# Keeping all engines of the first layer in source order, and taking its softmax one tile at a time, in a two-layer encoder on one core

## The chip, the core and the metric

The kernel runs on one core of a Trainium2 chip. A core has TensorE (PE, matrix products; its weight loads are listed as PEld), VectorE (DVE), ScalarE (ACT), GpSimd (POOL) and SyncE (SP), which here only issues transfers. All but SP and the transfers work from on-chip memory; each engine has its own list of instructions, and semaphores tie the lists together. The metric is the device time of one execution, in microseconds (us); lower is better.

## The reference

Input x has 512 tokens of 1024 features, in fp32. Two layers follow one another, each with its own weights:

```python
def reference(x, ...):
    for i in range(2):
        hn = rms_norm(x, norm_gain[i])
        y = mixer_a(hn, ...) if i == 0 else mixer_b(hn, ...)
        x = x + y
```

`mixer_a` projects hn to q, k and v for three dilation groups and to a gate, 16 heads of 64. q and k are normalised a head at a time. Each group is a window attention with a bias by relative distance (dilations 1, 4 and 16; 64 places of the group on each side). The three softmaxes are merged by their denominators, so that they can be computed as one softmax over all keys of the three groups. The result times silu(gate) goes through an output projection. `mixer_b` has one attention over a neighbourhood of an 8 x 64 grid with a bias in two dimensions, and the same gate and output projection.

## The kernel before

**Products.** Work goes by eight head pairs ("hc" in the code). A weight tile of up to 128 x 1024 fp32 (`wraw`, 8 slots) is loaded from HBM by SP, 512 KB at a time; some are first added to another one (POOL's adding DMA, line 184, or DVE, line 177). `split` (line 130) makes a high part `wh` (cast on ACT, line 133) and a low part `wl` (subtraction on DVE or POOL by turns, line 137), and a product is three matmuls, high x high, high x low and low x high (`mm3`, line 294). A job is the 128 x 512 piece of weights that one split gives: six matmuls of 512 columns in a `product`, or twelve at some places. `splits` keeps four splits queued ahead of the job that TensorE works on. Activations are split in the same way (hn_h and hn_l, and for the four sums and differences of quarters of hn in `mix`, mix_h and mix_l). From the second head pair on, projections are made from seven instead of eight block products (`main_a`): first the b11 product, then gate and v0 of the pair before, four products on mixed operands, and b21, with DVE and ACT adding the parts into rawq and rawk.

**Attention of layer A** (`attn_a`) for one pair, in the order of the code: q and k are turned (`tp`, `k_a`, `q_a`). Two passes (`scores(0)`, `scores(1)`) make scores ("log") of four tiles each. For each tile DVE adds the bias and takes minima (lines 935 and 946, into `p` and `mn`; the trace has four instructions for it), ACT takes exponents (959), DVE the reciprocal (769), ACT the normalisation (770), and DVE turns the tile in blocks of 32 into `pt` (883). SP then moves sixteen blocks, four at a time (`move`, line 891), so that probabilities lie transposed. `v_a` turns v; `bias_a` loads the next pair's bias (e<-l_d); `weigh` makes the products with v ("o"), and DVE multiplies the gate by them (790). A `y` tile goes to HBM and is read back and split at the end (yr<-y_d, 795 and 801).

**What sets the order.** TensorE's list is in source order. The source itself is woven: `main` yields after each block of matmuls, and `run` then calls `side` (the attention, startup and end work) until a due time. Time here is `clock`, a sum of the source's own estimates of the matmuls' lengths, in nanoseconds of TensorE. `later_on(d, job)` puts a job d further on; `yield d` lets the side rest for d; `yield "wait", key, d` rests until d after `stamp[key]`. All other engines' lists are put in order by a scheduler that simulates the program, except for the instructions wrapped in `tc.keep_in_program_order`, which stay in source order against each other. So the place of a DVE instruction need not be that of the source.

The relative bias of layer B is loaded at hc = 2 (`bias_rows`, 534), and its `fill` comes later by a timer of 4000 (537 to 542). At the start, `row_scale` ends the norm of layer A; then `scale_x`, `first_out` (head norms of the first q), `bias_lines`, `mix` and `q_a(0)` follow in `side`, while `main` goes through the first pair's projections.

Of the kernel before, what the change touches and what calls it, by code (L numbers as in the profile page):

```python
# [46 lines left out]
def tile_hybrid_encoder(  # L47
# [23 lines left out]

    def sb(t, off, dims):
        return bass.AP(t.tensor, t.offset + off, [t.ap[0]] + dims)
# [20 lines left out]
    nc.vector.memset(ones.bitcast(F32), 1.0)  # L94
    one = cp.tile([P, 1], F32, name="one")
    nc.vector.memset(one, 1.0)
# [14 lines left out]
    def rsqrt(eng, r, ss, n, scale):  # L111
# [6 lines left out]
        for _ in range(3):  # L118
            eng.tensor_mul(a[:, :n], r, r)  # L119
            if eng is nc.vector:  # L120
                eng.scalar_tensor_tensor(a[:, :n], a[:, :n], -0.5, v[:, :n], op0=ALU.mult, op1=ALU.mult)
                eng.scalar_tensor_tensor(r, a[:, :n], 1.5, r, op0=ALU.add, op1=ALU.mult)  # L122
                continue
# [6 lines left out]
    def split(raw, n):  # L130
        h = wp.tile([P, 512], F32R, tag="wh", name="wh", bufs=6)[:, :n]
        l = wp.tile([P, 512], F32R, tag="wl", name="wl", bufs=5)[:, :n]
        nc.scalar.copy(h, raw)  # L133
        turn[0] += 1
        a, b = pool[0]
        eng = nc.gpsimd if turn[0] * a % b < a else nc.vector
# [13 lines left out]
    class Plan:  # L150
# [28 lines left out]
        def add(self, at, dst, off):  # L179
# [4 lines left out]
                lambda: nc.gpsimd.dma_start(dst.tile, src(), accum_op=ALU.add)  # L184
            )

        def mixed(self, hc):
# [10 lines left out]
            for i in range(2):  # L198
                self.add(j + (2 if late else 3) + 2 * i, b11[i], b12[i].off)
                self.sum(j + (9 if late else 11) + 2 * i, t2[i], b11[i], b22[i], nc.vector)  # L200
# [48 lines left out]
    def load(raw):  # L249
# [4 lines left out]
        if not begun:  # L254
            nc.sync.dma_start(dst[:, :512], src[:, :512])
            begun.append(load_x(1, 2))
            dst, src = dst[:, 512:], src[:, 512:]
        nc.sync.dma_start(dst, src)
# [82 lines left out]
    def project(stat_h, stat_l, n, evac, guard, need=None, after=None):  # L341

        acc = {i: ps_acc.tile([P, 512], F32, tag="acc", name="acc") for i in range(4)}
        for k in range(KT):
# [11 lines left out]
            if after:  # L356
                yield ("xn",)
# [10 lines left out]
    def squares(v, ss, i, ns, on_act=True):  # L368
        sq = wk.tile([P, 512], F32, tag="sq", name="sq")[:, : ns * 64]
        if on_act:  # L370
            nc.scalar.activation(sq, v, AF.Square)  # L371
        else:
            nc.gpsimd.tensor_mul(sq, v, v)
        nc.vector.tensor_reduce(  # L374
            ss[:, i * ns : (i + 1) * ns], sq.rearrange("p (a b) -> p a b", b=64), axis=AX.X, op=ALU.add
        )
# [3 lines left out]
    def head_norm(raw, ss, ns, held):  # L380
# [3 lines left out]
        rsqrt(nc.vector, rs[:, : 4 * ns], ss[:, : 4 * ns], 4 * ns, 1.0 / DH)  # L384

        def scale():
            for i in range(4):
                by = rs[:, i * ns : (i + 1) * ns].unsqueeze(2).to_broadcast([P, ns, 64])
                v = raw[:, i, : ns * 64].rearrange("p (a b) -> p a b", b=64)
                m = nc.vector.tensor_mul(v, v, by)  # L390
                if held:
                    tc.keep_in_program_order(m)

        if held:
            later.append(scale)
        else:
            scale()
# [25 lines left out]
    def row_scale(ssq):  # L423

        rsqrt(nc.vector, rs_n, ssq, 4, 1.0 / D)
# [4 lines left out]
    def load_x(k0, k1):  # L430
        nc.sync.dma_start(x_all[:, k0:k1, :], xt[:, k0:k1, :])

    warm = cp.tile([P, 1], F32, name="warm")
    nc.vector.memset(warm, 0.0)
    nc.scalar.activation(warm, warm, AF.Exp)
    load_x(0, 1)
    nc.scalar.dma_start(ng, norm_gain)
# [12 lines left out]
    nc.scalar.dma_start(hg, head_gain)  # L450
    gk = cp.tile([P, 4], F32, name="gk")
    for i, (a, b) in enumerate(((0, 3), (1, 4), (2, 5), (6, 7))):
        nc.vector.scalar_tensor_tensor(
# [3 lines left out]
    def norm(layer, k, xk):  # L457
# [3 lines left out]
        nc.scalar.activation(h, xk, AF.Copy, scale=g)  # L461
        return nc.vector.scalar_tensor_tensor(l, xk, g, h.bitcast(F32), op0=ALU.mult, op1=ALU.subtract)

    def square_a(k):
# [3 lines left out]
        nc.scalar.activation(sq, x_all[:, k, :], AF.Square)  # L468
        if k:
            nc.gpsimd.tensor_add(st["ssq"], st["ssq"], sq)  # L470

    def scale_x():


        pa = spread()
        for k in range(KT):
            xk = x_all[:, k, :]
            nc.vector.scalar_tensor_tensor(xk, xk, ng[:, 0, k : k + 1], pa, op0=ALU.mult, op1=ALU.mult)

    def renorm(k):  # L480
        nc.scalar.copy(hn_h[:, k, :], x_all[:, k, :])
        (nc.gpsimd if k % 2 else nc.vector).tensor_sub(hn_l[:, k, :], x_all[:, k, :], hn_h[:, k, :].bitcast(F32))

    def mix():
# [6 lines left out]
        def put(n, src, eng):  # L491
            nc.scalar.copy(mix_h[:, n], src)
            eng.tensor_sub(mix_l[:, n], src, mix_h[:, n].bitcast(F32))

        nc.vector.tensor_sub(a, x21, x22)
        put(0, a, nc.gpsimd)
        yield 3000
        nc.vector.tensor_sub(b, a, x11)
        put(1, b, nc.vector)
        yield 4000  # L500
        nc.vector.tensor_add(b, b, x12)
# [940 lines left out]
```

## Time and profile before

| | |
|---|---|
| runs of the kernel before | 893.46 us median of three (890.31, 893.46, 900.19) |
| profiled execution | 896.53 us, its span 894.8 us |
| granted TensorE clock, mean | 0.973 |
| TensorE busy | 847.5 us, 95% of the span, 6611 matmuls |
| DVE busy | 650.4 us, 73% |
| ACT busy | 510.1 us, 57% |
| POOL busy | 311.4 us, 35% |
| data moved | 131.98 MB, 148 GB/s over the span |

Times of rows count from the start of the span. Layer A is 0 to about 594 us, layer B the rest. "Granted clock" is the share of TensorE's full speed that the chip's throttle let it have in that stretch; a stretch at 0.50 does half the work. In rows, "[x <-E]" says that the engine was idle for x us before the instruction, and that E ended this; "<-issue" is idle time for which the profile shows nothing. SPq rows are DMA issues, and their length is that of issuing, not of the transfer. All matmuls stand under the helper's line 288 and transposes under 292, so that they are told apart by the tiles' names.

### The profile page before, as it was taken

To read this page: it belongs to the slowest core of one execution; us is meant where nothing else is said; L and a number is where in the kernel's file an instruction comes from. 1 tells how busy PE (TensorE), PEld (TensorE's weight loads), DVE (VectorE), ACT (ScalarE), POOL (GpSimd) and SP (SyncE) were. 2 spreads that over 40 slices of the span, in tenths; PEclk is the share of its full clock that TensorE was granted. 3 is DMA by queue.
4 is the path that set the end of the run, shared out by engine and by line. 5 is a ranking of instruction groups with operands and counts; after the bars stand their busy time and mean duration, and the time that the engine had idled before them with its cause. 6 is when DMAs were issued, how large, how long until landed. Compare 5 with 4: busy or idle time off the path is not lost.

```text
span 894.8 us, 18174 instructions
## 1 busy us (share of the span) xinstructions
PE 847.5 (95%) x6611; PEld 700.7 (78%) x6611; DVE 650.4 (73%) x1641; ACT 510.1 (57%) x1066; POOL 311.4 (35%) x271
## 2 busy tenths in 40 slices
PE   9988999989997999989999898999999999999998
PEld 7766878868876778668878676778998988889776
DVE  6888995867866896886886886538576677766643
ACT  7656755835934845845845846436366446664540
POOL 6473442533432353343343334002222233222411
PEclk9998999989998999999999998989999999999999
DMA  9354575575474477475476472256235665455212
GB/s 344 117 109 101 134 198 127 122 219 129 115 210 141 107 187 185 106 218 141 107 200 180 105 235 80 65 172 215 95 127 138 168 185 156 136 146 146 92 48 95
DMA packets 56170, 131.98 MB, mean 148 GB/s; under 512 B 7184, under 2 KB 24528, under 8 KB 55952
## 3 DMA queue, kind: packets, MB, share of 16 engines
q1 hardware_dynamic: 49744, 108.78, 38.5%
q0 software_dynamic: 6048, 22.02, 14.6%
q8 instruction: 52, 0.85, 0.4%
q14 instruction: 38, 0.31, 0.1%
q10 hardware_dynamic: 288, 0.01, 0.0%
HBM read 111.73 MB, written 11.72 MB: 138 GB/s over the span
## 4 chain that ended last, share of the span: by engine, by line
PE 67%; DVE 11%; ACT 9%; DMA 6%; issue 4%; POOL 1%; SPq 1%; DVEq 0%; ACTq 0%; POOLq 0%
PE acc L288 55%; PE o L288 4%; PE log L288 4%; PE tp L292 4%; DVE wl L137 3%; DMA wraw<-in_w 2%; ACT p L770 2%; ACT p L1238 2%; ACT p L959 2%; DMA rp<-in_rpb 1%; ACT wh L133 1%; DVE rs L122 1%; DMA yr<-y_d 1%; DVE na L119 1%; ACT rawk L579 1%
## 5 line engine op out<-in xcount | busy, mean ns | idle before, releaser
L137 POOL TENSOR_TENSOR wl<-wraw,wh 128x512 fp32r<-128x512 f32 (+1 forms) x167 | 218.5, 1323 | 450.0 <-PE acc L288 229.3
L133 ACT CAST wh<-wraw 128x512 fp32r<-128x512 f32 (+1 forms) x360 | 210.0, 593 | 162.7 <-PE acc L288 141.8
L137 DVE TENSOR_TENSOR wl<-wraw,wh 128x512 fp32r<-128x512 f32 (+1 forms) x193 | 159.8, 830 | 66.3 <-PE acc L288 35.8
L288 PE MATMUL acc<-wh,hn_h 128*128 128x384 f32 (+1 forms) x488 | 190.1, 389 | 6.4 <-DVE rawq L657 2.3
L288 PE MATMUL acc<-wl,hn_h 128*128 128x384 f32 (+1 forms) x488 | 180.1, 369 | 0.6 <-DVE wl L137 0.4
L288 PE MATMUL acc<-wh,hn_l 128*128 128x384 f32 (+1 forms) x488 | 180.3, 369 | 0.0
L288 PEld LDWEIGHTS acc<-wh,hn_h 128*128 128x128 f32 x488 | 94.2, 193 | 26.5 <-issue 5.1
L288 PEld LDWEIGHTS acc<-wh,hn_l 128*128 128x128 f32 x488 | 93.7, 192 | 10.8 <-issue 0.4
L288 PEld LDWEIGHTS acc<-wl,hn_h 128*128 128x128 f32 x488 | 94.5, 194 | 9.2 <-DVE wl L137 0.9
L288 PE MATMUL acc<-wh,mix_h 128*128 128x512 f32 x224 | 89.6, 400 | 3.2 <-ACT wh L133 3.2
L288 PE MATMUL acc<-wl,mix_h 128*128 128x512 f32 x224 | 88.7, 396 | 2.8 <-DVE wl L137 1.7
L288 PE MATMUL acc<-wh,mix_l 128*128 128x512 f32 x224 | 88.2, 394 | 0.0
L288 PE MATMUL acc<-hn_h,wh 128*128 128x512 f32 x192 | 79.1, 412 | 0.2
L288 PE MATMUL acc<-hn_h,wl 128*128 128x512 f32 x192 | 75.4, 393 | 0.0
L288 PE MATMUL acc<-hn_l,wh 128*128 128x512 f32 x192 | 75.3, 392 | 0.0
L959 ACT ACTIVATE p<-p,mn 128x512 f32<-128x512 f32 (+1 forms) x64 | 44.9, 702 | 44.9 <-DVE mn L946 44.9
L770 ACT ACTIVATE p<-p,mn 128x512 f32<-128x512 f32 (+3 forms) x128 | 69.6, 588 | 0.0
L184 POOL DMA_DIRECT2D wraw<-in_w x42 | 37.3, 887 | 70.3 <-PE tp L292 17.9
L374 DVE TENSOR_REDUCE ss<-sq 128x4 f32<-128x256 f32 (+1 forms) x96 | 48.0, 503 | 16.3 <-ACT sq L371 8.9
L288 PE MATMUL acc<-y_h,wh 128*128 128x512 f32 x128 | 52.9, 414 | 4.1 <-ACT gt L610 4.0
L288 PEld LDWEIGHTS acc<-wh,mix_h 128*128 128x128 f32 x224 | 42.4, 189 | 14.2 <-ACT wh L133 4.3
L288 PEld LDWEIGHTS acc<-wl,mix_h 128*128 128x128 f32 x224 | 42.4, 189 | 13.3 <-DVE wl L137 3.2
(159 smaller groups left out, 1478.7 us busy)
## 6 DMA issues: line engine op xcount, KB each, us to landing
wraw<-in_w SPq DMA_DIRECT2D x95, 512.0 KB
wraw<-in_w POOLq DMA_DIRECT2D x42, 512.0 KB, 6.6
wraw<-in_w SPq DMA_DIRECT2D x38, 384.0 KB
pt<-pt SPq DMA_DIRECT2D x112, 64.0 KB
td<-tr SPq DMA_DIRECT2D x24, 224.0 KB
pt<-td SPq DMA_DIRECT2D x24, 224.0 KB
e<-l_d SPq DMA_DIRECT2D x32, 112.0 KB
e<-l_d SPq DMA_DIRECT2D x16, 128.0 KB
```

Source lines behind the costliest of these rows:

```text
L119: eng.tensor_mul(a[:, :n], r, r)
L122: eng.scalar_tensor_tensor(r, a[:, :n], 1.5, r, op0=ALU.add, op1=ALU.mult)
L133: nc.scalar.copy(h, raw)
L137: eng.tensor_sub(l, raw, h.bitcast(F32))
L184: lambda: nc.gpsimd.dma_start(dst.tile, src(), accum_op=ALU.add)
L288: nc.tensor.matmul(o, l, r, **kw)
L292: nc.tensor.transpose(o, i, ident)
L374: nc.vector.tensor_reduce(ss[:, i * ns : (i + 1) * ns], sq.rearrange("p (a b) -> p a b", b=64), axis=AX.X, op=ALU.add)
L579: nc.scalar.activation(dst, src, AF.Copy, scale=rs_n[:, i : i + 1])
L770: nc.scalar.activation(pr, pr, AF.Copy, scale=mn[:, 3:4])
L959: nc.scalar.activation(row, row, AF.Exp, bias=mn[:, 1:2], scale=-1.0, accum_out=mn[:, 2:3])
L1238: nc.scalar.activation(pr[:, o : o + n], pr[:, o : o + n], AF.Exp, bias=mn[:, 0:1], scale=-1.0, accum_out=mn[:, 2:3])
```

## The change

Four wrappers `vec`, `act`, `pol` and `syn` stand in for the engines everywhere. While `held[0]` is true, each instruction that goes through one of them is also kept in source order. It is set after the first `row_scale` and cleared when `main` has issued the last product of layer A:

```diff
+    held = [False]
+    class Ordered:
+        def __getattr__(self, name):
+            f = getattr(self.engine, name)
+            def call(*args, **kw):
+                m = f(*args, **kw)
+                return tc.keep_in_program_order(m) if held[0] else m
+            return call
+    vec, act, pol, syn = (Ordered(e) for e in (nc.vector, nc.scalar, nc.gpsimd, nc.sync))
...
     def main():
         for hc in range(NHC):
             yield from main_a(hc)
+        held[0] = False
```

As the list is then what the source says, the source now spells out the distance between steps that depend on one another, by timers and yields. The softmax goes a tile at a time:

```diff
-        def finish(hd, t, pr, row, mn):
-            normalise(row, mn)
-            turn(hd, t, pr, 4)
+        def least(n, tile_):
+            pr, row, mn = minima(*tile_)
+            later_on(1500, partial(exponents, row, mn))
+            later_on(2900, partial(normalise, row, mn))
+            later_on(3900, partial(turn, *tile_[:2], pr, 4))
         for u in range(2):
-            for n, (hd, t, pr, row, mn) in enumerate(scores(u)):
-                later_on(1300 * n, partial(exponents, row, mn))
-                later_on(1300 * n + 1300, partial(finish, hd, t, pr, row, mn))
+            for n, tile_ in enumerate(scores(u)):
+                later_on(400 + 900 * n, partial(least, n, tile_))
             if u:
                 stamp["scored", hc] = 0
                 for n in range(4):
-                    later_on(8500 + 1000 * n, partial(move, n))
-            yield 9500
+                    later_on(8000 + 2000 * n, partial(move, n))
+            yield 8500
         yield from v_a(hc)
-        yield "wait", ("pt", hc), 3000
+        yield "wait", ("pt", hc), 2500
         st["e", hc + 1] = bias_a(hc + 1)
-        yield "wait", ("pt", hc), 12500
+        yield "wait", ("pt", hc), 7500
```

Head norms (the reduce in `squares`, the squares themselves, the scales, `normed`) and the turns before the scores:

```diff
+        later_on(800, add) if held[0] else add()
+        later_on(800, partial(squares, *args)) if held[0] else squares(*args)
+            later_on(600 + 600 * i, partial(scale, i)) if held[0] else scale(i)
+        later_on(3000, go) if held[0] else go()
-        yield "wait", ("rawk", hc), 12000 if 0 < hc < NHC - 1 else 14000
+        yield "wait", ("rawk", hc), 8000 if hc < NHC - 1 else 11000
-        yield "wait", ("rawq", hc), 9000 if hc else 24000
+        yield "wait", ("rawq", hc), 8000
```

At the start, `scale_x` and `first_out` are woven together, a stamp each part, and `mix` comes before `bias_lines`; the products on mixed operands wait for the part that they use:

```diff
-        scale_x()
-        stamp["xn",] = 0
-        yield "wait", ("first",), 500
-        first_out()
-        yield 3000
-        bias_lines()
+        xs, parts = scale_x(), None
+        next(xs)
+        yield "wait", ("first",), 300
+        parts = first_out()
+        for _ in range(4):
+            next(parts)
+            yield 700
+            next(xs)
+            yield 700
+        next(parts, None)
+        for _ in xs:
+            yield 700
+        yield from mix()
+        yield from bias_lines()
         st["e", 0] = bias_a(0)
-        yield 2000
-        yield from mix()
-        stamp["mix",] = 0
         yield from q_a(0)
```

Beside that, `q_a` yields between its copies and subtractions, `mix` yields 1000 between its steps, the tiles of sums (`ss`) have three buffers instead of two, and `fill` is kept in order like the rest. The number of instructions on each engine is the same. Layer B's order is the scheduler's as before.

Where the instructions stand now is shown at three places. First SP at the third pair (hc = 2). Rows are transfers, destination <- source; `wraw` are weights, e0 and e12 the next pair's bias, `pt0<-pt` the moves. Before:

```order
L258 DMA wraw_2728<-in_w 128x1024
L810 DMA e0_2820<-l0_d_87 128x1x256 x2
L815 DMA e12_2821<-l12_d_88 128x1x224 x4
L891 DMA pt0_2431<-pt_98 32x512 x12
L258 DMA wraw_2771<-in_w 128x1024
L891 DMA pt0_2431<-pt_98 32x512 x4
L258 DMA wraw_2797<-in_w 128x1024
L258 DMA wraw_2835<-in_w 128x1024
L258 DMA wraw_2857<-in_w 128x1024
```

And after (L85 is the wrapper's call):

```order
L85 DMA wraw_2728<-in_w 128x1024
L85 DMA pt0_2434<-pt_98 32x512 x8
L85 DMA wraw_2767<-in_w 128x1024
L85 DMA pt0_2434<-pt_98 32x512 x4
L85 DMA wraw_2793<-in_w 128x1024
L85 DMA pt0_2434<-pt_98 32x512 x4
L85 DMA wraw_2821<-in_w 128x1024
L85 DMA e0_2837<-l0_d_87 128x1x256
L85 DMA e12_2838<-l12_d_88 128x1x224 x2
L85 DMA e0_2837<-l0_d_87 128x1x256
L85 DMA e12_2838<-l12_d_88 128x1x224 x2
L85 DMA wraw_2857<-in_w 128x1024
```

The moves stand ahead of the bias loads now, with a weight load between groups of four; before, they stood behind the bias loads, and four weight loads followed behind them in one run.

Second, DVE in the second pass of the same pair, from the last minima to the last turn (ISA is a minima instruction, STREAM_TRANSPOSE the turn). Before:

```order
L769 RECIPROCAL mn_2620<-mn_2620 128x1
L769 RECIPROCAL mn_2624<-mn_2624 128x1
L137 TENSOR_TENSOR wl_2670<-wraw_2502,wh_2669 128x512
L769 RECIPROCAL mn_2628<-mn_2628 128x1
L769 RECIPROCAL mn_2633<-mn_2633 128x1
L643 TENSOR_TENSOR rawq_2641<-acc_2642,rawk_158 128x512
L883 STREAM_TRANSPOSE pt_98<-p_2619 128x4x4x32
L643 TENSOR_TENSOR rawq_2641<-acc_2643,rawk_158 128x512
L883 STREAM_TRANSPOSE pt_98<-p_2623 128x4x4x32
L883 STREAM_TRANSPOSE pt_98<-p_2627 128x4x4x32
L137 TENSOR_TENSOR wl_2705<-wraw_2056,wh_2704 128x512
L883 STREAM_TRANSPOSE pt_98<-p_2632 128x4x4x32
```

And after:

```order
L85 ISA mn_2668 128x1
L85 RECIPROCAL mn_2633<-mn_2633 128x1
L85 TENSOR_TENSOR rawq_2622<-acc_2623,rawk_158 128x512
L85 TENSOR_TENSOR rawq_2622<-acc_2624,rawk_158 128x512
L85 STREAM_TRANSPOSE pt_98<-p_2632 128x4x4x32
L85 RECIPROCAL mn_2648<-mn_2648 128x1
L85 TENSOR_TENSOR wl_2701<-wraw_2056,wh_2700 128x512
L85 RECIPROCAL mn_2656<-mn_2656 128x1
L85 STREAM_TRANSPOSE pt_98<-p_2647 128x4x4x32
L85 RECIPROCAL mn_2668<-mn_2668 128x1
L85 STREAM_TRANSPOSE pt_98<-p_2655 128x4x4x32
L85 STREAM_TRANSPOSE pt_98<-p_2667 128x4x4x32
```

Before, the four reciprocals follow the four tiles' minima, and the turns stand together behind them. Now the first tile's turn stands ahead of the second tile's reciprocal, and the low part wl_2701 between two reciprocals.

On ACT at the same place (ACTIVATE p,mn is an exponent, ACTIVATE p a normalisation). Before:

```order
L959 ACTIVATE p_2619,mn_2620<-p_2619,mn_2620 128x512
L959 ACTIVATE p_2623,mn_2624<-p_2623,mn_2624 128x512
L621 COPY vt_2638<-vt_2638 128x64
L133 CAST wh_2669<-wraw_2502 128x512
L959 ACTIVATE p_2627,mn_2628<-p_2627,mn_2628 128x512
L959 ACTIVATE p_2632,mn_2633<-p_2632,mn_2633 128x512
L770 ACTIVATE p_2619<-p_2619,mn_2620 128x512
L770 ACTIVATE p_2623<-p_2623,mn_2624 128x512
L133 CAST wh_2684<-wraw_2502 128x512
L770 ACTIVATE p_2627<-p_2627,mn_2628 128x512
L133 CAST wh_2704<-wraw_2056 128x512
L770 ACTIVATE p_2632<-p_2632,mn_2633 128x512
```

And after:

```order
L85 ACTIVATE p_2632,mn_2633<-p_2632,mn_2633 128x512
L85 CAST wh_2660<-wraw_2483 128x512
L85 ACTIVATE p_2647,mn_2648<-p_2647,mn_2648 128x512
L85 ACTIVATE p_2632<-p_2632,mn_2633 128x512
L85 CAST wh_2679<-wraw_2483 128x512
L85 ACTIVATE p_2655,mn_2656<-p_2655,mn_2656 128x512
L85 ACTIVATE p_2667,mn_2668<-p_2667,mn_2668 128x512
L85 ACTIVATE p_2647<-p_2647,mn_2648 128x512
L85 CAST wh_2700<-wraw_2056 128x512
L85 ACTIVATE p_2655<-p_2655,mn_2656 128x512
L85 ACTIVATE p_2667<-p_2667,mn_2668 128x512
L85 CAST wh_2716<-wraw_2056 128x512
```

Exponents and normalisations of different tiles now alternate, and each cast has a fixed place among them; wh_2700, which wl_2701 above needs, stands behind two exponents and the normalisation of p_2647.

Third, DVE where the gate of the third pair meets the bias of layer B. Before:

```order
L390 TENSOR_TENSOR rawq_2641<-rawq_2641,rs_2889 128x512 x4
L537 TENSOR_SCALAR rp_3176<-rp_3176 128x248
L540 COPY lb_3218<-rp_3176 128x128
L790 TENSOR_TENSOR gt_2379<-gt_2379,o_2937 128x4x32
L790 TENSOR_TENSOR gt_2379<-gt_2379,o_2938 128x4x32
L790 TENSOR_TENSOR gt_2379<-gt_2379,o_2939 128x4x32
L790 TENSOR_TENSOR gt_2379<-gt_2379,o_2940 128x4x32
L662 TENSOR_TENSOR rawk_158<-rawk_158,acc_2700 128x512
```

And after, from the gate products on, and then where `fill` is:

```order
L85 TENSOR_TENSOR wl_2884<-wraw_2698,wh_2883 128x512
L85 TENSOR_TENSOR gt_2379<-gt_2379,o_2897 128x4x32
L85 TENSOR_TENSOR gt_2379<-gt_2379,o_2898 128x4x32
L85 TENSOR_TENSOR gt_2379<-gt_2379,o_2899 128x4x32
L85 TENSOR_TENSOR gt_2379<-gt_2379,o_2900 128x4x32
L85 TENSOR_REDUCE ss_2243<-sq_2890 128x8
```

```order
L85 TENSOR_TENSOR wraw_3218<-wraw_2698,wraw_2869 128x1024
L85 SCALAR_TENSOR_TENSOR gt_3192<-eg_3193,gt_3192 128x256
L85 TENSOR_TENSOR wl_3240<-wraw_2698,wh_3239 128x512
L85 TENSOR_SCALAR rp_3208<-rp_3208 128x248
L85 MEMSET lb_3299 128x376
L85 COPY lb_3299<-rp_3208 128x128
```

`fill` (rp, lb) stood ahead of the gate products (gt<-gt,o), and stands some forty rows behind them now, in the next pair's first pass.

317 lines of the change are left out of this document (163 added, 154 removed).

## The prediction

> **What bounds the kernel now.** I read the times first, then busy time by stage, TensorE's waits, and last the timeline around each wait.
>
> The stages (start:end, length, busy time and instructions of PE, PEld, DVE, ACT and POOL, granted clock, DMA share, GB/s):
> ```profile
> 58.00:594.00 536.00, 499.48 (x4641) 401.82 (x4642) 411.64 (x992) 318.83 (x618) 203.53 (x166) 0.96 0.56 145
> 424.20:486.10 61.90, 61.51 (x590) 50.07 (x590) 52.09 (x127) 40.63 (x79) 25.13 (x21) 1.00 0.66 169
> 486.10:562.00 75.90, 68.89 (x599) 54.97 (x599) 54.92 (x126) 46.34 (x84) 29.86 (x23) 0.93 0.48 136
> 436.00:459.00 23.00, 22.81 (x102) 18.61 (x102) 20.08 (x48) 17.69 (x36) 12.65 (x10) 1.00 0.57 132
> 594.00:895.00 301.00, 293.75 (x1749) 256.42 (x1747) 192.63 (x581) 153.66 (x387) 75.54 (x81) 1.00 0.47 140
> 509.40:512.80 3.40, 3.40 (x9) 2.49 (x10) 3.40 (x5) 3.28 (x7) 2.64 (x3) 0.50 0.26 88
> ```
> TensorE bounds it. The edit ends at 594, so all that it can win lies in the first row: 536.0 − 499.5 = 36.5 us idle, and a granted clock of 0.96, about 21 to 24 us of full speed (24 by adding up the stretches at 0.50, of 3.4 or 6.8 us, each worth half its length). Some 60 us in all. The second row is a head pair in which nothing is lost (0.4 us idle); the third one in which much is.
>
> What TensorE waits for between 0 and 594 (engine, line <- releaser: us, times, longest):
> ```profile
> PE tp L292 <- DVE gt L790: 7.0, 1, 7.0
> PE o L288 <- issue: 6.9, 2, 3.7
> PE tp L292 <- DVE rawq L390: 5.1, 1, 5.1
> PE acc L288 <- ACT gt L610: 4.0, 1, 4.0
> PE acc L288 <- ACT wh L133: 3.2, 2, 2.2
> PE acc L288 <- ACT rawk L579: 2.1, 1, 2.1
> PE acc L288 <- DVE wl L137: 2.1, 5, 0.7
> PE o L288 <- DMA pt<-pt: 2.1, 2, 1.4
> PE acc L288 <- POOL wl L137: 1.1, 2, 0.9
> ```
> Few and long: six accidents, not a steady rate. Each has its own cause, so I price them one by one; what follows an idle stretch at half clock is added to it.
>
> **The gains.** *The relative bias (7.0 + 3.4 of clock).* DVE row, then the load's issue on SP:
> ```profile
> 273.37 0.29 DVE L537 TENSOR_SCALAR rp<-rp 128x248 f32<-128x248 f32 x1 [10.07 <-DMA rp<-in_rpb]
> 260.29 0.58 SPq L534 DMA_DIRECT2D rp<-in_rpb  x1
> ```
> The load was issued behind five weight loads and landed 13.1 us later; DVE stood before it for 10.1 us, with the gate products behind it. In the changed order `fill` stands after the gate products, and its load behind one weight load: at 13.1 / 5 = 2.6 us for each of the five it lands after some 3 to 5 us, against the 4 that the timer allows and the rows of DVE between. 0 to 2 us of DVE may stay, behind which weight parts stand that are four jobs ahead. Gain 10 (8 to 10.4).
>
> *Startup (2.1 + 5.1, clock 5.1 = 12.3).*
> ```profile
> 57.87 0.18 DVE L122 SCALAR_TENSOR_TENSOR rs<-na,rs 128x32 f32<-128x32 f32 x1
> 58.54 9.04 DVE L122 SCALAR_TENSOR_TENSOR rs<-na,rs 128x32 f32<-128x32 f32 x1
> 61.46 2.71 POOL L493 TENSOR_TENSOR mix_l<-mixed,mix_h 128x1024 fp32r<-128x1024 f32 x1
> ```
> An operation that took 0.18 us just before took 9.04 while POOL ran mixes and splits back to back, and the scaled rawq behind it made TensorE wait 5.1. The change puts this reciprocal root and its scales ahead of mix(), and asks for the transposes later; that wait goes. The rawk copies (2.1 now) stand on ACT behind a cast of mix_h which itself waits for DVE: 1 to 4 us, and half clock. I leave 6 of the 12.3: gain 6 (2 to 10).
>
> *Code (6.9 in two).* SP, TensorE, and the packets of the instruction queue in 193.2 to 197:
> ```profile
> 188.49 3.38 SPq L258 DMA_DIRECT2D wraw<-in_w  x5
> 196.97 1.33 PE L288 MATMUL o<-pt,v 128*64 128x64 f32 x20 [3.74 <-issue]
> q8 instruction: 1, 0.02, 1.6%
> ```
> TensorE had nothing to wait for but its own instructions, whose packet stood behind five weight loads of 512 KB. With the moves spread out, one weight load stands between each four (order fence on SP): at most two ahead of such a packet. At 190–197 the head pair lost 8.9 with the weigh wait and clock, at 400 it lost 4.9 with clock. Gain 7.5 and 4.
>
> *Moves of the turned probabilities (pt), first head pair.*
> ```profile
> 131.61 0.55 PE L288 MATMUL o<-pt,v 128*64 128x64 f32 x8 [1.39 <-DMA pt<-pt]
> L891 SPq DMA_DIRECT2D pt<-pt x16: 507/588/1977, 446.5 to 460.8; - x16
> 440.60 5.79 SPq L815 DMA_DIRECT2D e<-l_d  x4
> ```
> That wait cost 1.39 + 0.70 and 1.7 of clock. The sixteen moves need 16 x 0.59 = 9.4 us of SP; before, they start behind the e loads, which hold SP 5.8 us for four. After, they start first, at 8 us behind the scores, a group each 2 us, and weigh asks for them 7.5 us behind the last: last issue 35.1 us after the first pass's scores plus 2 to 5 us of landing, against a first use near 38.2, so 0 to 2 are missing; I take 0.8. Gain 3 in the first pair; in three later pairs that waited for nothing 0.8 each is a loss, 2.4.
>
> *The end of layer A (4.0 + 1.7, clock 3.4).* Here ACT's gate stood behind two casts of y that waited for their load (3.2 of idle on ACT). Kept in order, those casts have about 5 us of slack. Gain 1 and 6.
>
> Sum of gains: 10 + 6 + 7.5 + 4 + 3 + 1 + 6 = 37.5.
>
> **The cost: softmax a tile at a time, in order.** The clean pass before, DVE and ACT, groups from 149 to 562 and single rows:
> ```profile
> L137 DVE TENSOR_TENSOR wl<-wraw,wh 128x512 fp32r<-128x512 f32 x95 | 88.6, 935 | 19.5 <-issue 9.6 <-PE acc L288 5.7 <-ACT sq L371 2.8
> L883 DVE STREAM_TRANSPOSE pt<-p 128x512 f32<-128x512 f32 x48 | 33.0, 693 | 4.2 <-ACT p L770 4.2
> L133 ACT CAST wh<-wraw 128x512 fp32r<-128x512 f32 x191 | 115.3, 617 | 58.5 <-PE acc L288 52.7 <-ACT k0h L738 1.8 <-POOL wl L137 1.6
> L959 ACT ACTIVATE p<-p,mn 128x512 f32<-128x512 f32 x36 | 25.7, 716 | 3.4 <-DVE mn L946 3.4
> L770 ACT ACTIVATE p<-p,mn 128x512 f32<-128x512 f32 x36 | 24.9, 715 | 0.0
> L137 POOL TENSOR_TENSOR wl<-wraw,wh 128x512 fp32r<-128x512 f32 x96 | 130.8, 1384 | 189.5 <-ACT wh L133 92.9 <-PE acc L288 56.6 <-DVE ss L374 6.8
> L620 ACT COPY vt<-acc 128x512 f32<-128x512 f32 x7 | 7.6, 1082 | 0.1
> 436.73 0.41 DVE L935 CUSTOM_DVE_ANT_0 p<-log,e 128x256 f32<-128x256 f32 x1
> 439.67 0.08 DVE L946 DVE_READ_ACCUMULATOR2_ANT mn<- 128x1 f32 x1
> 505.51 0.39 PE L288 MATMUL acc<-wl,mix_h 128*128 128x512 f32 x1
> 505.74 0.39 PE L288 MATMUL acc<-wh,mix_l 128*128 128x512 f32 x1
> 508.37 0.50 PE L288 MATMUL acc<-wh,mix_h 128*128 128x512 f32 x1 [2.24 <-ACT wh L133]
> ```
> The number of instructions stays; their places change. A job of six matmuls, 0.23 us apart, lasts 1.39 us and needs one cast (0.62, ACT) and one low part (0.65 on a free DVE, 1.3 on POOL, by turns); both are emitted four to five jobs ahead, a lead of about 6 us. In the four-tile pass all minima run in one piece (436.73 to 439.75, 0.75 a tile), then ACT runs exponents and normalisations (0.72 each) with casts put in wherever their operands are ready. Kept in order, a reciprocal waits on DVE for its exponent, a normalisation on ACT for its reciprocal, and the cast behind it on ACT, and then the low part on DVE or POOL, wait for both (order fences: wh_2700 behind the normalisation of p_2647, wl_2701 behind its reciprocal). I set these durations out in the new order over the two passes of a head pair, counting from the end of the first scores (the second end at 8.4). The cast at 18.0 gives POOL's low part at 19.3, due 18.8; the next, at 20.55, DVE's at 21.2, due 20.7; the third, held by the last normalisation to 23.2, POOL's at 24.5, due 22.6. So 0.5 + 0.5 + 1.9 = 2.9 us of TensorE in each of the seven head pairs with such passes, 20.5.
>
> Bounds: none at all (the clean pair had DVE busy for 20.1 of 23 us, and the lead covered it), or all of DVE's and ACT's work one after the other, 20.1 + 17.7 − 23 = 14.8 a pair. I take 2.9, near the worst rows of before: 2.24 in one wait at 508, and 5.7 of the 6.4 us in the three rows on wh and wl fell in softmax in three pairs. With 1.7 of clock those are 7.4 that the new 20.5 replace: net 13. Half clock: 1.7 a time, in half of seven pairs, 6.
>
> The last row of the first view shows what sets that: after 2.24 + 0.36 of idle near 508 the clock was 0.50 for 3.4 us. By the Trainium skill, TensorE: Matmul & The Clock Gate, Part 1 (What's actually happening), the gate closes only after an idle window of about 3.4 us; by that these stalls would cost no clock, the 6 would be 0, and the sum 6 lower. The trace disagrees, with half speed after 2.6 us of idle in two pieces, so the 6 stays.
>
> **Other edits.** The scales of queries and keys in steps of 600 and the reduces 800 later lengthen the chain to the transposes by 3 us and more; the waits before k_a and q_a shrink by 1 to 6, so they are asked for at about the same matmul; no term. Weight loads have 17 to 24 us from issue to cast in the new order, SP is at most 11 us behind: none late. Layer B keeps its order: 0 (its 301 us have 7.3 idle).
>
> **Sum.** −37.5 + 13.1 + 6 + 2.4 = −16.0, against the profiled execution's 896.5: 880.5. The median of the three runs shown is 3 lower than that execution, which would give 877.5; I say 879, between the two, 14.5 under the median.
>
> **The rivals.** Let x be the cost per head pair of the softmax in order, clock included; I took 3.8 (2.9 + 0.86). The time against before is 7x + 2.4 − 7.4 − 37.5, zero at x = 6.1.
> *The lead hides it (B).* The splits' 6 us absorb most of the hand-overs, as in the clean pair. For it: there DVE was just as full. Against: before, the casts were free to pass. x = 1.3 gives −33: 860.
> *In order, DVE and ACT stop each other (C), slower.* The place is the second pass of every pair: ACT waits at an exponent or normalisation for DVE, with up to three casts behind it, while DVE waits at a reciprocal with low parts behind it. For it: 37.8 us of work of the two in 23 us, and nothing may pass. Against: bound by my setting-out, whose delays add but do not grow from pass to pass, since over 35 of a pair's 62 us follow with less to do. It decides from x = 6.1; at 8, +13.5: 907. The Trainium skill, PSUM — Partial Sum Buffer, Engine vs sequencer instructions, states that the queues of ScalarE, VectorE and GpSimd are strict first-in, first-out, so a wait in the program's order holds all behind it; the trace agrees (10.07 us of DVE before rp, with the gate products behind).
> *The moves come too late (D).* Weigh now allows 7.5 us where it allowed 12.5, and all sixteen moves and the weight loads share SP's one queue. For it: the first pair's 3.8 us. If a wait of 3.1, clock included, stands in all seven pairs where I have 0.8, 16 more, the gain is used up: 893.
>
> **How the numbers follow.** Forecast 0.40, B 0.18, C 0.22, D 0.20. Forecast and rivals span 860 to 907, and each bound unknown (startup 2 to 10, moves 0 to 3.1, x 1.3 to 8) stays within; 860 to 908 leaves out half of C's upper side and a little of B, under 2 in 10. The forecast's own range is 870 to 888. A change of 1%, 8.9 us, is about what a measurement of this kernel can tell from none. Faster by more than that, under 884.5: B and about 0.32 of the forecast's 0.40, 0.50. Within 1%: the rest of it and 0.12 of D, 0.20. Slower: C and 0.08 of D, 0.30.
>
> **What would show it.** Right: no wait of tp before gt and rp, none of tp for rawq at startup, at most one code wait over 1 us; in each pair TensorE's waits for wh and wl together 2 to 4 us, in the 23 us after the first scores; waits for pt under 1 us. B shows as pairs of 62 us with no wl or wh wait; C as wl and wh waits over 6 us a pair and idle time on DVE before reciprocals; D as waits of o for DMA pt in every pair. The forecast is wrong if a new wait appears in a place that had none: rawk at startup beyond 4 us, or the y casts on ACT before k0h at the end.

## The result

The changed kernel takes 926.67 us (median of four runs, 924.76 to 928.77) against 893.71 (four runs): a ratio of 1.036, with a 95% interval of 1.030 to 1.043. Forecast were 879 us and a range of 860 to 908. It is slower by 33 us where 14.5 of gain were forecast.

### The profile page after: what moved, and what is told of

Its sections match the earlier page's. It is cut to its first block, busy times and chain, and to the rows that moved or that the text cites. A ratio compares the mean times of both kernels' runs of the same rounds, so it can differ in the third digit from the quotient of the medians.

```text
span 923.6 us, 18120 instructions
## 1 busy us (share of the span) xinstructions
PE 852.0 (92%) x6611; PEld 696.5 (75%) x6611; DVE 651.5 (71%) x1641; ACT 510.8 (55%) x1066; POOL 320.0 (35%) x271
## 4 chain that ended last, share of the span: by engine, by line
PE 53%; DVE 12%; issue 12%; ACT 11%; POOL 6%; DMA 4%; SPq 2%; POOLq 0%; ACTq 0%; DVEq 0%
PE acc L308 44%; ACT p L85 6%; PE o L308 4%; POOL wl L85 3%; PE tp L312 3%; ACT wh L85 2%; DVE p L85 2%; PE log L308 2%; SPq L85 2%; DVE wl L85 2%; DMA e<-l_d 2%; DVE na L85 1%; POOL wraw L85 1%; DVE pt L85 1%; DMA pt<-pt 1%
## 5 line engine op out<-in xcount | busy, mean ns | idle before, releaser
L85 POOL TENSOR_TENSOR wl<-wraw,wh 128x512 fp32r<-128x512 f32 (+1 forms) x167 | 227.6, 1367 | 492.6 <-ACT wh L85 236.0
L85 ACT CAST wh<-wraw 128x512 fp32r<-128x512 f32 (+1 forms) x360 | 205.3, 592 | 143.8 <-PE acc L308 134.5
L85 DVE TENSOR_TENSOR wl<-wraw,wh 128x512 fp32r<-128x512 f32 (+1 forms) x193 | 156.5, 814 | 93.5 <-ACT wh L85 41.3
L308 PE MATMUL acc<-wh,hn_h 128*128 128x384 f32 (+1 forms) x488 | 187.2, 384 | 12.9 <-ACT rawk L85 9.6
L85 ACT ACTIVATE p<-p,mn 128x512 f32<-128x512 f32 (+3 forms) x256 | 144.4, 588 | 69.6 <-DVE mn L85 69.1
L308 PE MATMUL acc<-wl,mix_h 128*128 128x512 f32 x224 | 91.1, 407 | 16.8 <-POOL wl L85 14.8
L85 DVE TENSOR_REDUCE ss<-sq 128x4 f32<-128x256 f32 (+1 forms) x96 | 46.5, 502 | 10.1 <-POOL sq L85 5.8
L85 DVE STREAM_TRANSPOSE pt<-p 128x512 f32<-128x512 f32 (+1 forms) x64 | 42.3, 671 | 15.2 <-ACT p L85 15.0
L308 PE MATMUL acc<-y_h,wl 128*128 128x512 f32 x128 | 51.1, 400 | 0.0
```

What stands on the lines that cost most here:

```text
L85: m = f(*args, **kw)
L308: nc.tensor.matmul(o, l, r, **kw)
```

## The profile after

The profiled execution of the changed kernel has a span of 923.6 us, 28.8 more than that of before. One event repeats in each head pair: the first matmul of the products with v (`o<-pt,rawk`), whose starts cut the span into four stages. The last column is what my terms give when they are put where they belong (softmax 3.8 in each pair; startup 6 and moves 3 in the first stage; code, bias and the old softmax waits in the second; the end's 7 in the third).

| stage | before | after | change | forecast |
|---|---|---|---|---|
| start to o of pair 1 | 128.1 | 145.4 | +17.3 | −5 |
| o of pair 1 to o of pair 7 | 401.8 | 403.9 | +2.1 | −4 |
| o of pair 7 to o of pair 8 | 56.1 | 66.8 | +10.7 | −7 |
| the rest, with layer B | 308.7 | 307.5 | −1.2 | 0 |

So the slow-down stands at the two ends of the layer; in the middle a new loss and the gains nearly cancel. TensorE's waits in the changed kernel, over the whole span:

```profile
PE acc L308 <- POOL wl L85: 14.8, 13, 4.6
PE acc L308 <- ACT rawk L85: 9.6, 3, 4.8
PE o L308 <- issue: 6.6, 4, 2.8
PE acc L308 <- ACT wh L85: 6.0, 13, 0.9
PE tp L312 <- ACT p L85: 5.3, 3, 3.8
PE acc L308 <- DVE wl L85: 4.6, 9, 2.3
PE tp L312 <- DVE k0l L85: 3.8, 3, 1.4
PE tp L312 <- DVE mk L85: 3.8, 1, 3.8
PE acc L308 <- ACT vt L85: 2.9, 1, 2.9
PE acc L308 <- ACT gt L85: 2.7, 1, 2.7
PE o L308 <- DMA pt<-pt: 1.7, 2, 1.2
```

Every instruction but TensorE's has the wrapper's line now, so tiles' names tell what it is. The waits on gt L790 (7.0), rawq (5.1) and much of pt are gone; wl, wh, rawk, mk and vt took their place, and the ones on wl and wh are many and short.

**The pairs.** TensorE in the second pass of the third pair, then ACT, then DVE at the same place:

```profile
257.04 0.50 PE L308 MATMUL acc<-wh,mix_h 128*128 128x512 f32 x1 [0.35 <-ACT wh L85]
258.40 0.50 PE L308 MATMUL acc<-wl,mix_h 128*128 128x512 f32 x1 [0.86 <-POOL wl L85]
260.38 0.50 PE L308 MATMUL acc<-wl,mix_h 128*128 128x512 f32 x1 [0.30 <-DVE wl L85]
262.43 0.49 PE L308 MATMUL acc<-wh,mix_h 128*128 128x512 f32 x1 [0.62 <-ACT wh L85]
263.79 0.50 PE L308 MATMUL acc<-wl,mix_h 128*128 128x512 f32 x1 [0.86 <-POOL wl L85]
```
```profile
257.61 0.71 ACT L85 ACTIVATE p<-p,mn 128x512 f32<-128x512 f32 x1
258.23 0.19 ACT L85 ACTIVATION_READ_ACCUMULATOR p<-p,mn 128x1 f32 x1
258.32 0.71 ACT L85 ACTIVATE p<-p,mn 128x512 f32<-128x512 f32 x1
258.93 0.60 ACT L85 CAST wh<-wraw 128x512 fp32r<-128x512 f32 x1
260.50 1.38 ACT L85 ACTIVATE p<-p,mn 128x512 f32<-128x512 f32 x2 [0.96 <-DVE mn L85]
261.78 1.12 ACT L85 CAST wh<-wraw 128x512 fp32r<-128x512 f32 x2
```
```profile
257.39 0.12 DVE L85 RECIPROCAL mn<-mn 128x1 f32<-128x1 f32 x1
259.64 0.69 DVE L85 TENSOR_TENSOR wl<-wraw,wh 128x512 fp32r<-128x512 f32 x1 [2.12 <-ACT wh L85]
260.25 0.16 DVE L85 RECIPROCAL mn<-mn 128x1 f32<-128x1 f32 x1
```

The same five waits stand in each of pairs 2 to 7, 0.35 + 0.86 + 0.30 + 0.62 + 0.86 = 2.99 us here. The last two fences show a ring through both engines. Two exponents have ended on ACT by 258.4. Their reciprocals stand on DVE behind the low part wl, which waits 2.12 us for a cast that stands on ACT behind those exponents and one normalisation. The next normalisation needs the reciprocal, so ACT idles 0.96 us with two more casts behind it. No engine is full: it is the places in the two lists.

**The start.** SP, ACT and POOL:

```profile
44.20 0.42 SPq L85 DMA_DIRECT2D mk<-in_maskc  x1
85.13 2.17 SPq L85 DMA_DIRECT2D l_d<-mk  x5
88.07 3.96 SPq L85 DMA_DIRECT2D e<-l_d  x6
92.08 4.83 SPq L85 DMA_DIRECT2D wraw<-in_w  x2
```
```profile
54.01 1.05 ACT L85 CAST mix_h<-mixed 128x1024 fp32r<-128x1024 f32 x1 [4.19 <-DVE mixed L85]
...
56.01 0.68 ACT L85 ACTIVATE rawk<-acc,rs_n 128x512 f32<-128x512 f32 x1
60.79 1.04 ACT L85 CAST mix_h<-mixed 128x1024 fp32r<-128x1024 f32 x1 [4.10 <-DVE mixed L85]
61.74 0.68 ACT L85 ACTIVATE rawk<-acc,rs_n 128x512 f32<-128x512 f32 x1
```
```profile
107.02 0.86 POOL L85 DMA_DIRECT2D wraw<-in_w  x1 [9.69 <-DMA wraw<-in_w]
107.58 1.59 POOL L85 TENSOR_TENSOR wl<-wraw,wh 128x512 fp32r<-128x512 f32 x1
```

For 41 us SP issued nothing: it stood at the transfer of mk, which DVE writes only behind mix now, with weight loads behind it. POOL's adding load then waited 9.69 us for one of those weights, with the low part behind it for which TensorE waited 4.6. On ACT the copies of rawk stand behind casts of mix_h that wait for DVE. TensorE's waits for rawk, mk and low parts in this stage add up to about 20 us, where the kernel before waited 7.2 (rawk 2.1, rawq 5.1). Half clock came with them: from 58 us to the first o the granted clock is 0.90, before it was 0.93, some 4 us of the 17.3 (estimated: the stretch's 87.5 and 70.1 us, times what is missing from 1).

**The end.** ACT's copy of vt, and DVE and POOL ahead of it:

```profile
577.03 1.08 ACT L85 COPY vt<-acc 128x512 f32<-128x512 f32 x1 [3.10 <-issue]
```
```profile
569.30 0.17 DVE L85 TENSOR_TENSOR na<-rs 128x16 f32<-128x16 f32 x1
569.51 1.45 DVE L85 SCALAR_TENSOR_TENSOR na<-na,nv 128x16 f32<-128x16 f32 x1
571.00 1.52 DVE L85 SCALAR_TENSOR_TENSOR rs<-na,rs 128x16 f32<-128x16 f32 x1
572.55 1.50 DVE L85 TENSOR_TENSOR na<-rs 128x16 f32<-128x16 f32 x1
...
575.02 1.94 DVE L85 TENSOR_TENSOR y_l<-yr,y_h 128x512 fp32r<-128x512 f32 x2
```
```profile
569.33 1.60 POOL L85 TENSOR_TENSOR y_l<-gt,y_h 128x512 fp32r<-128x512 f32 x1 [7.15 <-ACT y_h L85]
570.89 3.12 POOL L85 TENSOR_TENSOR y_l<-yr,y_h 128x512 fp32r<-128x512 f32 x2
```

vt and the y read back share a buffer (tag "tr"). The copy of vt starts 0.07 us after DVE's last low part of that y (575.02 + 1.94), and the gate stands on ACT behind vt and the casts and copies that follow it. In this stage TensorE waits 2.8 for code, 2.9 for vt, 2.7 for the gate and 4.4 in two for p, the last softmax; before, it waited 4.0 for the gate and 2.2 in four for p. The granted clock is 0.89 instead of 0.93, some 3 us more by the same estimate. The wait for p is between 4.0 and 4.7 us in every run of the changed source below, held or free, so holding is not its cause; what is, no run separates.

## The experiments

The theory: the loss comes from single instructions that stand at the head of a list kept in order and wait there, with work behind them that is ready. The rival: the new spacing of the source costs (later requests, one tile at a time), in whatever order. For each run the ratio to before with its interval, or the times where intervals don't decide, and the stages of the profile.

**Holding given up, in parts.** A second flag separates the hold from the timers:

```diff
-                return tc.keep_in_program_order(m) if held[0] else m
+                return tc.keep_in_program_order(m) if kept[0] else m
```

All free (the method returns m; what was held before stays so):

> The changed source with all its spacing, one tile of softmax at a time, but no instruction held beyond those that were held before. Theory 1: the five waits per pair for wh and wl go with the rest, 880 to 898. Theory 2: 915 to 929, with the waits for wl and wh still there.

884.44 us, ratio 0.991 (0.988 to 0.994): 42 us under the changed kernel, by the order alone, and under before. Stages 132.8, 384.8, 56.8, 307.9. The rival falls as the cause of the whole. In the first stage it keeps a part: 132.8 is still 4.7 us more than before, with nothing held. Of the waits for wh and wl, 8.9 us are left over the layer, not 25.4.

Held only from the first `k_a` on (`kept[0] = True` moved behind `q_a(0)`), and held except for the last pair (`kept[0] = False` ahead of `main_a(7)`):

> The changed kernel, with the engines held in source order only from the first pair's k_a on; the startup's new source stays, but the scheduler orders it. Theory 1 (a queue kept in order stands at its head, and what is ready behind it waits): the three waits for rawk (9.6 us), the one for mk (3.8), the POOL wl at 109 (4.6) and their half clock go, the first scores come at about 88 instead of 96.7 and the first o at about 131 instead of 145, so 910 to 914. Theory 2 (it is the new spacing in the source that costs, in whatever order): 922 to 929.

> The changed kernel, with the hold given up before the last pair's projections. Theory 1: the waits for vt (2.9) and gt (2.7) at 578 and 582 and the clock behind them go, and some of the last softmax's 3: 916 to 921. Theory 2: 922 to 929.

918.88, a smaller gain than expected, and 920.54, as expected. The first comes to its first o at 139.2, 6 us earlier: rawk (4.9 in one) and a wait of 4.4 for the first softmax are left. The second has 56.6 in the third stage (10.2 less), but 411.5 in the second (7.6 more): a gain at one end came back as waits elsewhere.

One engine free at a time:

```diff
-    vec, act, pol, syn = (Ordered(e) for e in (nc.vector, nc.scalar, nc.gpsimd, nc.sync))
+    act, pol, syn = (Ordered(e) for e in (nc.scalar, nc.gpsimd, nc.sync))
+    vec = nc.vector
```

> The changed kernel with DVE left to the scheduler, and ACT, POOL and SP held. If DVE's held order is the cause (a reciprocal behind a low part that waits for its cast, which waits on ACT for the normalisation before it), the waits for wh and wl fall by more than half and the time to 895 to 908. If ACT's order is the cause: 918 to 929, with the waits in the pairs as they were.

> The changed kernel with ACT left to the scheduler, and DVE, POOL and SP held. If the casts that stand behind softmax on ACT make the five waits a pair, these waits go (3 us idle and about 4.2 with the restart, five pairs and more: 21 to 27 us), and the three waits for rawk at startup (9.6 and half clock) shrink: 888 to 898. If the reciprocals behind low parts on DVE make them, they stay: 915 to 925.

> The changed kernel with SP left to the scheduler but for the moves and what was held before. If SP's order holds weight loads up at startup only (mk to l_d), the first o comes 6 to 10 us earlier, the pairs stay at 68: 914 to 920. If SP's order matters nowhere: 924 to 929; if it is also what keeps code waits low, these rise to 9 us or more.

DVE free: 889.25, ratio 0.998 (0.994 to 1.001). ACT free: 905.68, 1.012 (0.997 to 1.028). From pair 1 to 7 they take 382.3 and 386.6 against 403.9, so freeing either one opens the ring; neither guess of a single guilty engine was right. The rest of DVE's lead is at the ends (135.0 and 60.0 against 140.9 and 68.1). SP free was wrong altogether: 938.18, ratio 1.049 (1.026 to 1.072), first o at 147.8. Its SP and DVE rows say why:

```profile
84.13 1.72 SPq L556 DMA_DIRECT2D l_d<-mk  x4
...
93.36 12.74 SPq L279 DMA_DIRECT2D wraw<-in_w  x2
```
```profile
108.23 0.36 DVE L85 CUSTOM_DVE_ANT_0 p<-log,e 128x192 f32<-128x192 f32 x1 [6.70 <-DMA e<-l_d]
111.60 0.48 DVE L85 CUSTOM_DVE_ANT_1 p<-log,e,mn 128x256 f32<-128x256 f32 x1 [3.00 <-DMA e<-l_d]
```

The transfers of mk go out as late as in the changed kernel (84.13 against 85.13), since held DVE makes mk late. TensorE's wait of 4.6 for the low part is gone (no wait for one of POOL's is over 0.9), so that one was SP's order; but the bias arrives later still, and held DVE stands 9.7 us for it in the first softmax, where it stood 3.2. Freeing DVE alone does not cure it either: with SP held, mk's transfers go out at 76.8, and TensorE waits 6.8 us for the low part. What decides is the place of `bias_lines` in the source, as the next run shows. In the pairs SP free lost 7 us more, with waits for pt of 7.5 us.

**The order of the source at the start.** `bias_lines` ahead of `mix`, all held:

```diff
-        yield from mix()
         yield from bias_lines()
+        yield from mix()
```

> The changed kernel, all held, with bias_lines ahead of mix as it was before. Theory 1 for SP: SP stood from 44 to 85 at the transfers of mk to l_d, with four weight loads behind; they go out earlier, the waits for mk (3.8) and for POOL wl (4.6) go, and DVE's wait for e (3.2): 912 to 918. If the startup's loss is all ACT's and DVE's own: over 922, with the rawk waits as large as now.

919.56, a smaller gain than expected. The first o comes at 135.7, 9.8 earlier: mk's transfers go out at 56.8, the waits for mk and for the low part at 109 are gone, and rawk's fell from 9.6 to 0.7 us too, since the casts of mix now follow the copies. But new waits for low parts stand at 77 and 84 (3.3 and 4.9), and 3.3 came back in the pairs (407.2) with code waits of 10.0 us.

**The ring.** Only the reciprocals move, 1000 ahead, still held:

```diff
-            later_on(2900, partial(normalise, row, mn))
+            later_on(1900, lambda: vec.reciprocal(mn[:, 3:4], mn[:, 2:3]))
+            later_on(2900, lambda: act.activation(row, row, AF.Copy, scale=mn[:, 3:4]))
```

> The changed kernel, all held, with each tile's reciprocal put 1000 further ahead, so that it stands ahead of the low part (wl_2701 in the changed kernel) that it stood behind; nothing else moves. If the waits in the pairs come from that loop (cast on ACT, low part on DVE, reciprocal behind it on DVE, normalisation on ACT, next cast behind it), the waits of 0.30, 0.62 and 0.86 at the pass's end go, 2 to 2.5 us a pair: pairs of 65 to 66.5 us instead of 68.4, 910 to 917. If held order as such is the cost, whichever rows stand where, pairs of 68 and 922 to 929.

899.39, ratio 1.006 (1.002 to 1.009): 27 us from moving four instructions of 0.16 us a pass, where 10 to 17 were expected. All five waits went, not three. In the profiles 21.2 us of it lie between the o of pair 1 and of pair 7, and 4.0 ahead of the first o. On DVE the third and the fourth reciprocal stand ahead of the low part now:

```profile
249.09 0.16 DVE L85 RECIPROCAL mn<-mn 128x1 f32<-128x1 f32 x1
249.17 0.67 DVE L85 TENSOR_TENSOR rawq<-acc,rawk 128x512 f32<-128x512 f32 x1
249.76 0.70 DVE L85 STREAM_TRANSPOSE pt<-p 128x512 f32<-128x512 f32 x1
250.38 0.12 DVE L85 RECIPROCAL mn<-mn 128x1 f32<-128x1 f32 x1
250.99 0.69 DVE L85 TENSOR_TENSOR wl<-wraw,wh 128x512 fp32r<-128x512 f32 x1 [0.48 <-ACT wh L85]
```

Four pairs, from the second to the sixth o, in the changed kernel and then in this one:

```profile
206.94:479.75 272.81, 253.62 (x2353) 200.40 (x2353) 211.89 (x507) 162.60 (x317) 115.98 (x88) 1.00 0.64 156
```
```profile
201.59:460.15 258.56, 249.45 (x2353) 202.41 (x2352) 211.56 (x507) 161.30 (x317) 115.17 (x88) 0.99 0.68 164
```

14.25 us in four pairs, 3.6 each, for the same number of instructions: 2.5 each of TensorE's idle time (19.2 against 9.1 us in all) and 1.0 of its busy time (253.62 against 249.45). The idle is less than 2.99 a pair because waits for code and pt grew in the place of some. The busy time is what a wait costs beyond its idle: from 257.04 to 264.36 there are fifteen starts in 7.32 us, where fifteen steps of 0.23 are 3.45 and the waits between are 2.64, so 1.2 us more for four waits, 0.3 each. The granted clock stayed at 1.00 (0.99 with the ring open).

Two other cures:

> The changed kernel, all held, with exponents, normalisation and turn 2000, 4200 and 5700 behind the minima instead of 1500, 2900 and 3900, and moves from 9000 in steps of 1700. If spacing in the source can stand in for the scheduler, waits for wh and wl in the pairs fall below 1.5 us a pair: 908 to 916. If the loop only moves: pairs of 67 to 69, 920 to 930.

> The changed kernel, all held, with splits queued five ahead instead of four (one buffer more for wh and for wl, and one weight slot less, 7, to make the room). A lead longer by 1.39 us should take the waits of 0.26 to 0.86 in the pairs away if they are a lead that falls a little short: pairs of 64 to 65 us instead of 68, 905 to 912. If the loop between ACT and DVE grows with the lead, pairs of 67 to 69 and 920 to 930. Startup as now.

Wider spacing gave 919.74 us: wh and wl fell to between 1.2 and 1.4 us a pair, as asked, but the time did not follow; waits for rawq (7.0) and pt (4.6) took their place. A longer lead for the splits gave 932.28: wh and wl fell to between 0.4 and 1.7 us a pair, but rawq (13.6 in eight) and DMA waits of o (11.3) came, and a weight slot was missing, so it doesn't tell what the lead alone is worth. That the waits are a lead that falls short was my reading; lengthening it didn't help as the reciprocals did.

**What the tile at a time is worth.** Nothing held, softmax, moves and waits of weigh as before:

> The changed source with nothing held, and the softmax of before (four tiles' minima at once, the old distances, moves and waits of weigh). If the tile at a time is worth nothing by itself, 880 to 890, as with all free; if the gain of all free comes from it, 890 to 898; if it costs, under 880, with the waits for pt (5.6 us) gone.

894.92, ratio 1.002 (0.999 to 1.005), against 0.991 all free: 10 us, and 397.2 against 384.8 from pair 1 to 7. So the new softmax, together with its moves and the waits of weigh, is a gain where order is free. Held, its places were a loss, of which the reciprocal's was 27 us; the old softmax was not run held.

**The parts together.**

> Nothing held beyond what was held before, and the reciprocal 1000 earlier in the source. If the reciprocal's place mattered only because DVE was held, no change against all free: 881 to 888. If it is a better order in itself: under 880.

> All held, the reciprocal early and bias_lines ahead of mix. If the startup's loss is the two heads (SP at mk's transfers, ACT at the casts of mix ahead of the copies of rawk) and adds to the loop's: the first o at 133 to 137, pairs of 64 to 65, 888 to 893. If the time won at startup is given back in the next pairs, as it was with bias_lines alone: 894 to 900.

> As the one before, with the hold given up before the last pair's projections. If the end's 11 us are the held heads there: 8 to 11 less than the one before, 878 to 884. If it was the new order of the source: no change.

> The reciprocal early, held only from the first k_a to the last pair. If the held order in the pairs costs nothing without the loop, the time is that of all free or better, 878 to 886; if holding is worth something by itself, under 876; if the first softmax suffers as it did when only the start was free (53.6 us from the first scores to the first o), 886 to 894.

All free with the early reciprocal: 888.39, 0.996 (0.993 to 0.998), no better than without it. All held with reciprocal and bias_lines: 888.66, 0.996 (0.994 to 0.998), as expected; it takes 378.7 from pair 1 to 7, the least of all. Giving up the hold for the last pair: 889.37, no change; the third stage fell from 67.4 to 57.9, but pair 7 before it grew from 62.6 to 73.7, with a wait for rawk of 5.8 us. Start and end free: 893.85, as expected of a first softmax that suffers: its scores wait 4.4 us for DVE's minima, and pair 7 takes 73.6 here too.

**The end, and the best order.** For the first, all low parts of y read back are made on DVE:

```diff
-        (vec if hc % 2 else pol).tensor_sub(l, src, h.bitcast(F32))
+        vec.tensor_sub(l, src, h.bitcast(F32))
```

> All held, the reciprocal early, bias_lines ahead of mix, and all low parts of y read back made on DVE, none on POOL. If POOL's work beside DVE's small operations makes the late end, these take about 0.2 us each, the wait for vt (3.0) falls under 1.5, and from o of the seventh pair to o of the eighth it takes 63 to 65 us instead of 67.4. If it is the order alone, vt waits 3 us or more, 67 to 69.

The small operations, 1.45, 1.52 and 1.50 us in the changed kernel (1.44, 1.50 and 1.49 in the run without this edit), took 0.17 or 0.18 each, with POOL idle:

```profile
532.29 0.17 DVE L85 SCALAR_TENSOR_TENSOR na<-na,nv 128x16 f32<-128x16 f32 x1
532.50 0.18 DVE L85 SCALAR_TENSOR_TENSOR rs<-na,rs 128x16 f32<-128x16 f32 x1
532.71 0.17 DVE L85 TENSOR_TENSOR na<-rs 128x16 f32<-128x16 f32 x1
```

That part is shown, in one execution (886.83 us). But the stage has 65.7 instead of 67.4, 1.7 of some 10 and less than expected: TensorE waits 1.2 for vt and 3.3 for the gate, 4.5 where it was 5.7. DVE now makes five low parts of y there instead of two (5.0 us instead of 1.9), which uses up most of what the small operations won. With DVE and ACT free the stage takes 56, so the rest is their order; with DVE alone free it takes 60.0, with ACT alone 68.1, and which rows make it was not separated.

DVE and ACT free, POOL and SP held, and then the same with bias_lines ahead of mix:

> The changed source with POOL and SP held, DVE and ACT left to the scheduler. If the loss is DVE's and ACT's order and nothing else, the time is that with all free, 882 to 888; if SP's held order adds to it through code waits (11 us with DVE free or ACT free alone, 3.8 with all free), 888 to 896; if it is worth something (moves at even distance), under 880.

> DVE and ACT left to the scheduler, POOL and SP held, bias_lines ahead of mix. If mk's transfers at the head of SP still hold weights up there (POOL wl waits of 5.6 us with DVE and ACT free), 877 to 882. If that wait has another cause: 883 to 889.

885.77 (0.991, 0.988 to 0.995), then 879.81, ratio 0.984 (0.980 to 0.988): faster than both kernels (1.6% under the one before). The first is what all free gave; all free with `bias_lines` first was not run, so whether holding POOL and SP adds anything is not shown. The wait for POOL wl fell from 6.0 to 0.4 and that for rawk from 5.8 to 1.7; the first o comes at 125.8. What is left there between 0 and 640, the longest rows:

```profile
PE o L309 <- issue: 11.0, 5, 3.4
PE tp L313 <- ACT p L807: 4.7, 2, 3.8
PE tp L313 <- DVE rawk L417: 3.5, 1, 3.5
```

## Why the prediction was wrong

*The softmax in order* (2.9 us of idle a pair): right in place and in kind, and near in size; 2.99 were measured in six pairs, not seven, and 3.6 a pair came back when the ring was opened. That 2.9 and 2.99 agree is in part luck: I had three waits of 0.5, 0.5 and 1.9 for low parts, and there are five of 0.30 to 0.86, two of them for casts. The link that closes the ring, a low part on DVE ahead of the next reciprocal, stood in the order shown but not in my account. My 0.86 of half clock a pair was wrong in kind: the clock stayed at 1.00, and the restart after each wait (0.3 each) took its place. The idle is in five pieces over 7 us, where in the kernel before 2.6 us of idle within 3.3 came just ahead of the half clock. Rival C asked for more than 6.1 a pair and did not happen; the kernel is slower by other places.

*Startup* ("Gain 6"): the failed step, 22 us off with the first pair's. I priced the reciprocal root and the rawk copies, and gave no term to `bias_lines` behind `mix`, though the diff shows it. SP's list stood 41 us at mk; with the bias first the stage is 9.8 shorter even when all is held. I had foreseen the cast ahead of the rawk copies and put it at 1 to 4 us; it was 9.6 in three, the sign that I had named for a wrong forecast. With all free 4.7 us of the stage's loss stay, so they belong to the new order of the source and not to holding.

*The end* ("Kept in order, those casts have about 5 us of slack. Gain 1 and 6"): failed, 18 us off. The wait of the gate came back as 2.9 on vt and 2.7 on gt, and 2.8 for code and 2.2 more for the last softmax, to neither of which I had given a term here, came beside it. I had looked at the casts on ACT, not at DVE's low parts behind them, which give vt its buffer.

*Code* ("Gain 7.5 and 4"): failed. 6.6 us were waited in four instead of 6.9 in two. Three of the four (0.7, 1.5 and 1.6) came while SP was issuing four or five bias loads, which the change had put behind the moves, and the longest, 2.8, behind two weight loads, no more than the "at most two" that I had counted on. In the twenty kernels this wait is between 0.6 and 11.8 us, and where it is low the wait for pt or e is high (with five splits ahead 0.6, 5.9 and 5.4; all free 3.8 and 5.6 for pt; the best order 11.0 and none for pt): a gain in one of them is not a gain for o. That the one hides the other was not tried by itself.

*The relative bias* ("Gain 10"): right. No wait of tp on gt is left, and DVE did not wait for rp. *Moves of pt*: rival D failed, 1.7 us in all; but the first pair still waits 1.2 where I had 0.8 (2.1 before), and one later pair 0.5 where I had three of 0.8. *Layer B*: unchanged within 1.2 us.

## What to carry to other kernels

When lists are fixed by hand, read for every instruction that waits what is ready behind it, on each engine and on the queue of transfers; a tiny instruction behind the wrong neighbour closed a ring, and moving it won 27 us. Gains read from waits of the old order are only gains if the new order makes no new heads: price what was moved behind what, SP's list included, before taking them. And free first: with the same source, the scheduler's order for DVE and ACT was better than the hand's, while holding SP and POOL beside it changed nothing that could be measured (885.77 against 884.44).

## What the runs showed of the hardware

Small DVE operations of 0.17 us with two operands in on-chip memory took 1.45 to 1.52 us while POOL subtracted, and 0.17 or 0.18 when POOL did not. The Trainium skill, SBUF — State Buffer, Who interferes with whom, says that a DVE instruction with two inputs in SBUF, the on-chip memory, contends with a GpSimd instruction that reads SBUF, over a port pair that is an exclusive lock. The trace agrees: the three operations end at 570.96, 572.52 and 574.05, and POOL's three subtractions of about 1.6 us each run from 569.33 to 574.01, so one of these is the price of one operation of 0.17.

Waits short and apart (2.99 us in five within 7 us) left the granted clock at 1.00; in the kernel before, 2.6 us of idle within 3.3 were followed by 3.4 us at 0.50.
